# Block chunks of weights: four sums side by side, one rounding and one split

## The chip, the cores and the metric

The kernel runs on one core of a Trainium2 chip. The metric is the device time of one execution in microseconds. A profiled execution gives a span (first to last instruction of the program) and a trace of every engine: PE (matmul, with its weight loads as PEld), DVE (elementwise), ACT (copies, casts, activations), POOL and SP (which issues the loads from HBM).

## The reference

Two layers of a decoder trunk on 256 tokens of width 2048, all in float32. Layer 0 mixes stick-breaking attention and an SSD scan, layer 1 a causal mixture of dilated windows; each layer ends with a gated ConvFFN of inner width 5632.

```python
for layer in range(DEPTH):
    hn = rms_norm(h, mix_norm_w[layer])
    ...
    h = h + mix.astype(h.dtype)
    f = conv_ffn(rms_norm(h, ffn_norm_w[layer]), ffn_w_gate[layer], ffn_w_up[layer],
                 ffn_conv_w[layer], ffn_conv_b[layer], ffn_w_down[layer])
    h = h + f.astype(h.dtype)
return rms_norm(h, final_norm_w)
```

What the change touches is the product of activations with weights in two places: the value projection of layer 1 (`hn @ w_in`, its last third, in `odd`) and the last down projection (`... @ w_down` of layer 1, in `finish`).

## The kernel before

All weights stream once from HBM in chunks of 512 KB (128 partitions by 1024 floats). Each product is made of three terms: activations and weights are each held as a rounded part (high, of type fp32r) and a rest (low), and high*high, high*low and low*high are summed. So each chunk that lands in a `raw` buffer is prepared by ACT, which writes the rounded part, and DVE, which writes the rest, before PE may use it.

There are two kinds of chunk.

- A **plain chunk** goes through `prep` (lines 148 to 168): one load (L164), one cast on ACT of 1024 columns (L166), one subtraction on DVE (L167). PE uses it in `chan` (L242) or, in `finish`, in `plain` (L586).
- A **block chunk** goes through `pair_prep` (lines 473 to 506). It holds four blocks of 256 columns, and the product of a 2 by 2 block matrix is formed in seven block products in place of eight (`seven`, L534; 21 matmuls of 256 columns, with three terms each). Three blocks are used as they are (B11, B21, B22), and four sums of blocks (T1 to T4) are formed on DVE first (L492, L495, L496) in a buffer `tf`. PE takes them in the order B11, B21, B22, T1, T3, T2, T4.

Block chunks are used 51 times. 24 of them are in `odd`: its loop over p from 0 to 3 projects queries and keys of four heads in 16 plain chunks, with a chunk of the values after each second plain one; for p = 1, 2 and 3 these are block chunks. I number them 0 to 23 (0 to 7 for p = 1, and so on), and call the two plain chunks that PE uses just ahead of block chunk 9 by 9a and 9b. Attention for the heads (`dilated`: L850 to L883) and the values' sums (`combine`: L546 to L556) run between them, in generators that are stepped once a chunk. The other 27 are in `finish`, where plain and block chunks alternate.

Three pools set how far preparation runs ahead: `raw` has 4 buffers, `hl` 3 (one per chunk of either kind), and `ts` 2, for block chunks alone. `tf` has one. In a block chunk before the change, `hl` holds the B blocks (high, low) and T4; `ts` holds T1 to T3. A buffer is handed out again when its last reader is done, so the cast of B (L491) waits for PE to be done with the chunk that had the `hl` buffer, and a load waits for the last instruction that reads the `raw` buffer it gets.

The code does not set the order on an engine directly: a scheduler of the language places the instructions of each engine when the program is built, by its own estimate of when each can start, and decides there which buffer each chunk gets. On the chip each engine then runs its list strictly in that order, and SP issues loads in its own order.

Of the kernel before, what the change touches and what calls it, by code (L numbers as in the profile page):

```python
# [9 lines left out]
F32 = mybir.dt.float32  # L10
# [3 lines left out]
ALU = mybir.AluOpType  # L14

P = 128
T = 256
# [55 lines left out]
class Trunk:  # L73
# [399 lines left out]
    def pair_prep(self, src, off=OFF):  # L473

        nc = self.nc
        v = nc.vector
        raw = self.wraw.tile([P, CH * 272], F32, tag="raw", name=self.nm("raw"))[:, : 4 * T]
        hl = self.whl.tile([P, CH * 544], F32R, tag="hl", name=self.nm("hl"))  # L480
        ts = self.ph.tile([P, 128 + 6 * T], F32R, tag="ts", name=self.nm("ts"), bufs=2)
        cut = lambda t, o, n: t[:, off + o * T : off + (o + n) * T]
        b = cut(hl, 0, 3), cut(hl, 3, 3)
        t123 = cut(ts, 0, 3), cut(ts, 3, 3)
        t4 = cut(hl, 6, 1), cut(hl, 7, 1)
        nc.sync.dma_start(raw, src)
        blk = lambda t, i, n=1: t[:, i * T : (i + n) * T]
        two = lambda t: t.rearrange("p (i c) -> p i c", c=T)
        f = self.ph.tile([P, 4 * T], F32, tag="tf", name=self.nm("tf"), bufs=1)
        f123, f4 = blk(f, 0, 3), blk(f, 3)  # L490
        nc.scalar.copy(b[0], blk(raw, 0, 3))  # L491
        v.tensor_tensor(  # L492
            two(blk(f123, 0, 2)), two(blk(raw, 1, 2)), blk(raw, 3).unsqueeze(1).broadcast_to([P, 2, T]), ALU.subtract
        )
        v.tensor_tensor(blk(f123, 2), blk(raw, 2), blk(f123, 0), ALU.add)  # L495
        v.tensor_tensor(f4, blk(raw, 0), blk(f123, 2), ALU.subtract)  # L496
        v.tensor_tensor(b[1], blk(raw, 0, 3), b[0].bitcast(F32), ALU.subtract)  # L497
        nc.scalar.copy(t123[0], f123)  # L498
        nc.scalar.copy(t4[0], f4)
        v.tensor_tensor(t123[1], f123, t123[0].bitcast(F32), ALU.subtract)  # L500
        self.lo = v.tensor_tensor(t4[1], f4, t4[0].bitcast(F32), ALU.subtract)
        one = lambda t, i: (blk(t[0], i), blk(t[1], i))
        return {
            "B21": one(b, 0), "B11": one(b, 1), "B22": one(b, 2),
            "T1": one(t123, 0), "T3": one(t123, 1), "T2": one(t123, 2), "T4": t4,
        }

    def part(self, x, p, tt):
        return x[:, p * T + tt * P : p * T + (tt + 1) * P]
# [859 lines left out]
```

## Time and profile before

| | us |
|---|---|
| three runs | 2176.47, 2177.75, 2178.99 (median 2177.75) |
| the profiled execution | 2177.32 |
| its span, first to last instruction | 2175.5 |
| mean granted TensorE clock | 0.999 |
| `odd`, p = 1 to 3 (24 block chunks) | about 1155 to 1365 of the span |
| `finish`, block chunks 24 to 50 | about 1985 to 2160 of the span |

Every row of the timeline gives start, duration, engine, line, operation, what it writes and reads, and how often; in brackets stands the idle time ahead of it and what ended that. PE's matmuls are pipelined: the duration of one is its latency, and the distance between the starts of two is what it costs.

### The profile page before, as it was taken

The numbers are of one execution on the slowest core, as the hardware profiler recorded it, in microseconds if no ns is written. First come the engines' busy times: TensorE is split into PE (matmuls) and PEld (weight loads), VectorE is DVE, ScalarE is ACT, GpSimd is POOL, SyncE is SP. The second block draws the span as 40 slices with busy tenths as digits, with TensorE's granted clock in tenths as the row PEclk, the third lists the DMA queues.
The fourth block names the chain that finished last, engine by engine and source line by source line (L and its number), as shares of the span: only waits on it lengthen the run. The fifth ranks groups of instructions, "written<-read, shape, count | busy, mean of one in ns | idle before, by whom it ended". The sixth has DMA issues, their size and how long they took to land.

```text
span 2175.5 us, 34570 instructions
## 1 busy us (share of the span) xinstructions
PE 2164.5 (99%) x13335; PEld 1935.9 (89%) x13335; DVE 1595.9 (73%) x2518; ACT 1195.4 (55%) x1782; POOL 96.9 (4%) x107
## 2 busy tenths in 40 slices
PE   9999999999999999999999999999999999999998
PEld 8888888888888888888889999888888888888998
DVE  8688776766666665555578888767676767688997
ACT  7566554655555554444455655546555555555554
POOL 0000000101010100000000000000010101000000
PEclk9999999999999999999999999999999999999999
DMA  7754566666666666666665556666666666666665
GB/s 253 242 175 146 174 184 191 189 193 194 193 195 194 193 194 195 194 193 194 193 182 183 175 176 192 178 192 187 188 193 195 193 194 194 194 200 203 208 203 169
DMA packets 117717, 417.59 MB, mean 192 GB/s; under 512 B 13072, under 2 KB 15408, under 8 KB 117552
## 3 DMA queue, kind: packets, MB, share of 16 engines
q1 hardware_dynamic: 116352, 412.48, 62.4%
q8 instruction: 104, 1.70, 0.3%
q0 software_dynamic: 576, 2.10, 0.3%
q10 hardware_dynamic: 624, 0.81, 0.1%
q14 instruction: 61, 0.50, 0.1%
HBM read 413.22 MB, written 2.11 MB: 191 GB/s over the span
## 4 chain that ended last, share of the span: by engine, by line
PE 96%; DVE 2%; DMA 1%; ACT 0%; issue 0%; DVEq 0%
PE acc L242 77%; PE acc L586 5%; PE acc L519 3%; PE aux L534 3%; PE acc L534 2%; PE acc L252 1%; PE aux L519 1%; DMA raw<-in_wodv 1%; DVE hl L167 1%; PE acc L203 1%; PE acc L259 1%; PE aux L881 0%; PE acc L211 0%; PE aux L211 0%; PE aux L849 0%
## 5 line engine op out<-in xcount | busy, mean ns | idle before, releaser
L242 PE MATMUL acc<-x,hl 128*128 128x512 f32 (+1 forms) x7680 | 1324.3, 333 | 1.7 <-DVE hl L167 1.6
L242 PEld LDWEIGHTS acc<-x,hl 128*128 128x128 f32 x7680 | 1157.8, 188 | 152.0 <-DVE hl L167 2.2
L167 DVE TENSOR_TENSOR hl<-raw,hl 128x1024 fp32r<-128x1024 f32 x713 | 872.4, 1224 | 499.5 <-ACT hl L166 493.1
L166 ACT CAST hl<-raw 128x1024 fp32r<-128x1024 f32 x713 | 748.4, 1050 | 701.5 <-PE acc L242 476.5
L242 PE MATMUL acc<-act,hl 128*128 128x512 f32 (+1 forms) x1408 | 239.5, 332 | 0.0
L242 PEld LDWEIGHTS acc<-act,hl 128*128 128x128 f32 x1408 | 211.7, 188 | 27.7
L242 PE MATMUL acc<-o,hl 128*128 128x256 f32 (+1 forms) x1024 | 176.0, 333 | 0.0
L242 PEld LDWEIGHTS acc<-o,hl 128*128 128x128 f32 x1024 | 154.2, 188 | 20.1 <-ACT das L857 0.2
L301 ACT COPY ev<-acc 128x256 f32<-128x256 f32 x242 | 89.9, 373 | 140.1 <-PE acc L242 138.0
L747 POOL TENSOR_TENSOR cv<-cv,rbc 128x256 f32<-128x256 f32 x88 | 93.8, 1084 | 852.7 <-ACT cv L746 852.7
L586 PE MATMUL acc<-hl,act 128*128 128x256 f32 x924 | 110.4, 276 | 0.0
L586 PEld LDWEIGHTS acc<-hl,act 128*128 128x128 f32 x924 | 107.9, 188 | 0.3
L302 DVE TENSOR_TENSOR ev<-acc,ev 128x256 f32<-128x256 f32 x242 | 101.1, 420 | 3.1 <-ACT ev L301 1.7
L498 ACT CAST ts<-tf 128x768 fp32r<-128x768 f32 x51 | 42.7, 837 | 36.9 <-DVE tf L495 36.8
L519 PE MATMUL acc<-hl,act 128*128 128x512 f32 x264 | 60.0, 389 | 0.0
L491 ACT CAST hl<-raw 128x768 fp32r<-128x768 f32 x51 | 42.6, 836 | 29.9 <-issue 18.2
L519 PEld LDWEIGHTS acc<-hl,act 128*128 128x128 f32 x264 | 49.5, 188 | 10.3
L497 DVE TENSOR_TENSOR hl<-raw,hl 128x768 fp32r<-128x768 f32 x51 | 48.7, 954 | 4.2 <-ACT hl L491 4.0
L500 DVE TENSOR_TENSOR ts<-tf,ts 128x768 fp32r<-128x768 f32 x51 | 48.6, 953 | 2.2 <-ACT ts L498 2.2
L492 DVE TENSOR_TENSOR tf<-raw 128x512 f32<-128x512 f32 x51 | 35.2, 690 | 18.9 <-DMA raw<-in_wodv 15.0
L757 DVE TENSOR_TENSOR ev<-ev,cv 128x256 f32<-128x256 f32 x88 | 38.3, 437 | 10.2 <-POOL cv L747 1.5
L309 POOL MEMSET pad<- 128x2 f32 (+1 forms) x8 | 0.5, 100 | 928.1 <-DVE sum L122 928.1
(253 smaller groups left out, 1556.4 us busy)
## 6 DMA issues: line engine op xcount, KB each, us to landing
raw<-in_wg SPq DMA_DIRECT2D x176, 512.0 KB, 3.9
raw<-in_wu SPq DMA_DIRECT2D x176, 512.0 KB, 3.8
raw<-in_wd SPq DMA_DIRECT2D x176, 512.0 KB, 3.6
raw<-in_wev SPq DMA_DIRECT2D x76, 512.0 KB, 4.1
raw<-in_wod SPq DMA_DIRECT2D x64, 512.0 KB, 3.9
raw<-in_wevo SPq DMA_DIRECT2D x32, 512.0 KB, 3.6
raw<-in_wodv SPq DMA_DIRECT2D x32, 512.0 KB, 3.6
raw<-in_wodo SPq DMA_DIRECT2D x32, 512.0 KB, 4.3
```

The costliest lines, as they stand in the source:

```text
L166: nc.scalar.copy(hi, raw)
L167: self.lo = nc.vector.tensor_tensor(lo, raw, hi.bitcast(F32), ALU.subtract)
L242: self.mm = self.nc.tensor.matmul(accs[nt][:, :n], hl[w][:, k, nt * P : (nt + 1) * P], xs[k0 + k][:, :n], start=start and k == w == 0, sto ...
L301: nc.scalar.copy(t, acc[:, T:])
L302: nc.vector.tensor_tensor(t, acc[:, :T], t, ALU.add)
L497: v.tensor_tensor(b[1], blk(raw, 0, 3), b[0].bitcast(F32), ALU.subtract)
L498: nc.scalar.copy(t123[0], f123)
L500: v.tensor_tensor(t123[1], f123, t123[0].bitcast(F32), ALU.subtract)
L519: self.nc.tensor.matmul(row.rearrange("p (j c) -> p j c", c=T), self.part(a[k], p, tt), self.both(hl, w, k), start=start and i == k == 0, ...
L534: self.nc.tensor.matmul(to, x[p], w[b][q], start=n == 0 and i in start, stop=n == 2 and i in stop, skip_group_check=alone or i in m,)
L586: mm(block(accs, tt, j) if own is None else own[:, :T], x, both(hl, w, k)[:, j], start=first, stop=stop and k == 1 and i == 2 and j == hal ...
L747: nc.gpsimd.tensor_tensor(c, c, self.rbc, ALU.mult)
```

## The change

The four sums now lie side by side in the `hl` buffer, high and low, and are rounded by one ACT cast of 1024 columns and split by one DVE subtraction of 1024 columns. The B blocks move to `ts`. The products and their operands' values are the same.

```diff
-        b = cut(hl, 0, 3), cut(hl, 3, 3)
-        t123 = cut(ts, 0, 3), cut(ts, 3, 3)
-        t4 = cut(hl, 6, 1), cut(hl, 7, 1)
+        t = cut(hl, 0, 4), cut(hl, 4, 4)
+        b = cut(ts, 0, 3), cut(ts, 3, 3)
         nc.sync.dma_start(raw, src)
...
         nc.scalar.copy(b[0], blk(raw, 0, 3))
         v.tensor_tensor(
-            two(blk(f123, 0, 2)), two(blk(raw, 1, 2)), blk(raw, 3).unsqueeze(1).broadcast_to([P, 2, T]), ALU.subtract
+            two(blk(f, 0, 2)), two(blk(raw, 1, 2)), blk(raw, 3).unsqueeze(1).broadcast_to([P, 2, T]), ALU.subtract
         )
-        v.tensor_tensor(blk(f123, 2), blk(raw, 2), blk(f123, 0), ALU.add)
-        v.tensor_tensor(f4, blk(raw, 0), blk(f123, 2), ALU.subtract)
+        v.tensor_tensor(blk(f, 2), blk(raw, 2), blk(f, 0), ALU.add)
+        v.tensor_tensor(blk(f, 3), blk(raw, 0), blk(f, 2), ALU.subtract)
         v.tensor_tensor(b[1], blk(raw, 0, 3), b[0].bitcast(F32), ALU.subtract)
-        nc.scalar.copy(t123[0], f123)
-        nc.scalar.copy(t4[0], f4)
-        v.tensor_tensor(t123[1], f123, t123[0].bitcast(F32), ALU.subtract)
-        self.lo = v.tensor_tensor(t4[1], f4, t4[0].bitcast(F32), ALU.subtract)
+        nc.scalar.copy(t[0], f)
+        self.lo = v.tensor_tensor(t[1], f, t[0].bitcast(F32), ALU.subtract)
```

Of the changed kernel's lines, L489 is the cast of B and L495 its subtraction (L491 and L497 before), L490, L493 and L494 form the sums (L492, L495, L496 before), and L496 and L497 are the merged cast and subtraction. Lines behind `pair_prep` stand six lower: L528 is L534 before.

The list of every engine but SP and POOL changes, since the cast of B no longer needs an `hl` buffer and the scheduler places it, and what follows it, earlier. Three places:

**ACT, from block chunk 8 to 9b.** Before: `raw1678` holds the weights of block chunk 8, and `hl1673`, `hl1683` and `hl1685` are the plain chunks 8b, 9a and 9b.

```order
L166 CAST hl1673_11771<-raw1672_11770 128x1024
L546 COPY tc1661_11718<-acc1565_11045 128x256
L491 CAST hl1679_11798<-raw1678_11797 128x768
L499 CAST hl1679_11798<-tf1681_11801 128x256
L166 CAST hl1683_11833<-raw1682_11832 128x1024
L551 ACTIVATE vw1662_11719<-vw1662_11719,rcol1455_10383 128x512
L556 ACTIVATE vw1663_11720<-vw1663_11720,rcol1455_10383 128x512
L857 ACTIVATE das1668_11747,dam1669_11748<-das1668_11747,dam1669_11748 128x128 x2
L857 ACTIVATE das1668_11747,dam1669_11748<-das1668_11747,dam1669_11748 128x256 x2
L166 CAST hl1685_11854<-raw1684_11853 128x1024
```

After, over the same stretch; `raw1692` holds the weights of block chunk 9.

```order
L166 CAST hl1673_11755<-raw1672_11754 128x1024
L540 COPY tc1661_11702<-acc1565_11045 128x256
L496 CAST hl1679_11782<-tf1681_11785 128x1024
L489 CAST ts1694_11878<-raw1692_11876 128x768
L545 ACTIVATE vw1662_11703<-vw1662_11703,rcol1455_10383 128x512
L550 ACTIVATE vw1663_11704<-vw1663_11704,rcol1455_10383 128x512
L166 CAST hl1683_11815<-raw1682_11814 128x1024
L851 ACTIVATE das1668_11731,dam1669_11732<-das1668_11731,dam1669_11732 128x128 x2
L851 ACTIVATE das1668_11731,dam1669_11732<-das1668_11731,dam1669_11732 128x256 x2
L166 CAST hl1685_11836<-raw1684_11835 128x1024
```

The cast of block chunk 9 stands ahead of the casts of 9a and 9b and of the values and exponentials; before, it stood behind 9b. On DVE a little earlier the same happens: before, the list at block chunk 8 runs L492, L495 (its first sums), L167 of 8a; after, it runs L495 (low half of block chunk 8's B), L490, L493, L167 of 8a.

**DVE, block chunk 5.** Before; `raw1632` is block chunk 5's, `hl1625` and `hl1627` are 5a and 5b, `das` and `dam` belong to the attention's softmax.

```order
L850 TENSOR_TENSOR das1614_11379<-aux1616_11381,consts_93 128x384
L167 TENSOR_TENSOR hl1625_11455<-raw1624_11454,hl1625_11455 128x1024
L850 TENSOR_TENSOR das1614_11379<-aux1617_11385,consts_93 128x384
L492 TENSOR_TENSOR tf1635_11510<-raw1632_11506 128x512
L853 TENSOR_REDUCE dam1615_11380<-das1614_11379 128x2 x2
L495 TENSOR_TENSOR tf1635_11510<-raw1632_11506,tf1635_11510 128x256
L496 TENSOR_TENSOR tf1635_11510<-raw1632_11506,tf1635_11510 128x256
L860 RECIPROCAL dam1615_11380<-dam1615_11380 128x4
L863 TENSOR_TENSOR das1614_11379<-das1614_11379,dam1615_11380 128x2x128
L863 TENSOR_TENSOR das1614_11379<-das1614_11379,dam1615_11380 128x2x256
L167 TENSOR_TENSOR hl1627_11476<-raw1626_11475,hl1627_11476 128x1024
```

After, the same stretch.

```order
L490 TENSOR_TENSOR tf1635_11500<-raw1632_11496 128x512
L493 TENSOR_TENSOR tf1635_11500<-raw1632_11496,tf1635_11500 128x256
L495 TENSOR_TENSOR ts1634_11498<-raw1632_11496,ts1634_11498 128x768
L844 TENSOR_TENSOR das1614_11371<-aux1616_11373,consts_93 128x384
L844 TENSOR_TENSOR das1614_11371<-aux1617_11377,consts_93 128x384
L167 TENSOR_TENSOR hl1625_11445<-raw1624_11444,hl1625_11445 128x1024
L847 TENSOR_REDUCE dam1615_11372<-das1614_11371 128x2 x2
L494 TENSOR_TENSOR tf1635_11500<-raw1632_11496,tf1635_11500 128x256
L854 RECIPROCAL dam1615_11372<-dam1615_11372 128x4
L857 TENSOR_TENSOR das1614_11371<-das1614_11371,dam1615_11372 128x2x128
L857 TENSOR_TENSOR das1614_11371<-das1614_11371,dam1615_11372 128x2x256
L167 TENSOR_TENSOR hl1627_11466<-raw1626_11465,hl1627_11466 128x1024
```

Three instructions that read block chunk 5's weights now stand ahead of the scores, of 5a and of the softmax's maximum (L853, now L847).

**PE, block chunk 1.** Before; `hl1572` is the plain chunk 1a, and the products of block chunk 1 come 32 matmuls later.

```order
L534 MATMUL aux1564_11044<-hl1568_11048,x1236_8750 128x256 x3
L242 MATMUL acc1551_10970<-x1321_9516,hl1572_11083 128x512
L242 MATMUL acc1551_10970<-x1321_9516,hl1572_11083 128x256
L242 MATMUL acc1551_10970<-x1322_9521,hl1572_11083 128x512
L242 MATMUL acc1551_10970<-x1322_9521,hl1572_11083 128x256
```

After; `ts1581` is block chunk 1.

```order
L528 MATMUL aux1564_11044<-hl1568_11048,x1236_8750 128x256 x3
L242 MATMUL acc1551_10970<-x1321_9516,hl1572_11081 128x512
L242 MATMUL acc1552_10971<-x1321_9516,hl1572_11081 128x512
L528 MATMUL acc1565_11045<-ts1581_11134,x1240_8778 128x256 x3
L528 MATMUL aux1563_11043<-ts1581_11134,x1241_8783 128x256
L242 MATMUL acc1551_10970<-x1321_9516,hl1572_11081 128x256
L242 MATMUL acc1551_10970<-x1322_9521,hl1572_11081 128x512
```

Two products with the high half of 1a and four of block chunk 1 stand ahead of the first product with 1a's low half. Elsewhere PE's list is the same but for the buffers' names.

SP issues the same loads in the same order, but some get another `raw` buffer and so wait for other work. Block chunk 9's load waited for the split of 8b (L167) and now waits for the last sum of block chunk 8 (L494); the same holds for block chunks 5, 6, 7, 13, 14, 15, 17, 21, 22 and 23 with the one ahead of each. Block chunk 8's load waited for the split of 7b and now waits for that of 7a.

More of the change, by code (lines that the diff above doesn't have):

```diff
@@ L489, in pair_prep @@
         f = self.ph.tile([P, 4 * T], F32, tag="tf", name=self.nm("tf"), bufs=1)
-        f123, f4 = blk(f, 0, 3), blk(f, 3)
         nc.scalar.copy(b[0], blk(raw, 0, 3))
         v.tensor_tensor(
-            two(blk(f123, 0, 2)), two(blk(raw, 1, 2)), blk(raw, 3).unsqueeze(1).broadcast_to([P, 2, T]), ALU.subtract
+            two(blk(f, 0, 2)), two(blk(raw, 1, 2)), blk(raw, 3).unsqueeze(1).broadcast_to([P, 2, T]), ALU.subtract
         )
-        v.tensor_tensor(blk(f123, 2), blk(raw, 2), blk(f123, 0), ALU.add)
-        v.tensor_tensor(f4, blk(raw, 0), blk(f123, 2), ALU.subtract)
+        v.tensor_tensor(blk(f, 2), blk(raw, 2), blk(f, 0), ALU.add)
+        v.tensor_tensor(blk(f, 3), blk(raw, 0), blk(f, 2), ALU.subtract)
         v.tensor_tensor(b[1], blk(raw, 0, 3), b[0].bitcast(F32), ALU.subtract)
[L498 to L501, printed above, removed]
+        nc.scalar.copy(t[0], f)
+        self.lo = v.tensor_tensor(t[1], f, t[0].bitcast(F32), ALU.subtract)
         one = lambda t, i: (blk(t[0], i), blk(t[1], i))
[L503 to L506, printed above, removed]
+        out = {n: one(b, i) for i, n in enumerate(("B21", "B11", "B22"))}
+        return out | {n: one(t, i) for i, n in enumerate(("T1", "T3", "T2", "T4"))}
     def part(self, x, p, tt):
```

## The prediction

> **What bounds the kernel now.** I read the page's busy shares first, then the chain that ended last, then busy time by window for the two stages that the change touches.
>
> ```profile
> PE 2164.5 (99%) x13335; PEld 1935.9 (89%) x13335; DVE 1595.9 (73%) x2518; ACT 1195.4 (55%) x1782; POOL 96.9 (4%) x107
> PE 96%; DVE 2%; DMA 1%; ACT 0%; issue 0%; DVEq 0%
> core 0: us, PE busy (x) PEld busy (x) DVE busy (x) ACT busy (x) POOL busy (x), PEclk, DMA share, GB/s
> 1155.00:1365.00 210.00, 209.58 (x1409) 192.38 (x1408) 184.22 (x313) 125.21 (x225) 0.00 (x0) 1.00 0.59 182
> 1985.00:2160.00 175.00, 175.00 (x1485) 172.72 (x1484) 158.09 (x240) 99.79 (x137) 0.00 (x0) 1.00 0.65 201
> ```
>
> PE is busy 2164.5 of 2175.5 us and 96% of the last chain is PE. In the window of `odd` (first row) PE lacks 0.42 us of 210, in that of `finish` nothing, at full clock. The change leaves every matmul. So it can win only what PE waits for here, which the chain of waits in the window of `odd` gives (us in total, times, longest):
>
> ```profile
> DVE tf L492 <- DMA raw<-in_wodv: 15.0, 10, 3.1
> PEld acc L534 <- DVE hl L497: 0.7, 2, 0.4
> PEld acc L242 <- DVE ev L302: 0.4, 1, 0.4
> PE acc L534 <- DVE hl L497: 0.2, 1, 0.2
> PE acc L242 <- DVE ev L302: 0.2, 1, 0.2
> ```
>
> PE's four waits make 1.5 us. The 0.7 is the low half of B coming late at block chunks 8 and 16. The first row is as important: ten times DVE stood waiting at the head of its list for a block chunk's load, up to 3.1 us, and PE mostly had cover.
>
> **What the instructions cost.** Groups of one shape each, mean ns behind the bar:
>
> ```profile
> L167 DVE TENSOR_TENSOR hl<-raw,hl 128x1024 fp32r<-128x1024 f32 x713 | 872.4, 1224 | 499.5 <-ACT hl L166 493.1
> L497 DVE TENSOR_TENSOR hl<-raw,hl 128x768 fp32r<-128x768 f32 x51 | 48.7, 954 | 4.2 <-ACT hl L491 4.0
> L500 DVE TENSOR_TENSOR ts<-tf,ts 128x768 fp32r<-128x768 f32 x51 | 48.6, 953 | 2.2 <-ACT ts L498 2.2
> L501 DVE TENSOR_TENSOR hl<-tf,hl 128x256 fp32r<-128x256 f32 x51 | 21.4, 419 | 0.0
> L492 DVE TENSOR_TENSOR tf<-raw 128x512 f32<-128x512 f32 x51 | 35.2, 690 | 18.9 <-DMA raw<-in_wodv 15.0 <-DMA raw<-in_wd 3.0
> L498 ACT CAST ts<-tf 128x768 fp32r<-128x768 f32 x51 | 42.7, 837 | 36.9 <-DVE tf L495 36.8
> L499 ACT CAST hl<-tf 128x256 fp32r<-128x256 f32 x51 | 20.5, 403 | 1.1 <-DVE tf L496 1.1
> ```
>
> DVE's two subtractions cost 0.953 + 0.419 = 1.37 us; one of 1024 columns costs 1.22 as L167 does. ACT's two casts cost 0.837 + 0.403 = 1.24; one of 1024 costs 1.05 (the row of L166 at block chunk 1, below). That saves 0.15 us of DVE and 0.19 of ACT per block chunk, 51 times 7.6 and 9.7 us. **Both lie beside PE, so I cost the saving at nothing**, save where DVE was what PE waited for. The Trainium skill ("Perfetto Trace Analysis", section "Optimizing Scalar/DVE Operations") says that grouping helps if the engine is saturated, and that where it is not, but makes others wait, smaller instructions may let work finish sooner; by the first half the sum would be lower (rival C), by the second higher, and DVE's 184 of 210 us, with the ten waits above among its idle time, lies nearer to the second.
>
> **T123 comes later.** The merged cast waits for the fourth sum (0.42 us) and both operations are longer (0.21 and 0.27): T's low half is ready 0.5 to 0.9 us later. The tightest place is block chunk 1:
>
> ```profile
> 1166.35 0.96 DVE L500 TENSOR_TENSOR ts<-tf,ts 128x768 fp32r<-128x768 f32 x1 [0.44 <-ACT ts L498]
> 1169.01 1.18 PE L534 MATMUL acc<-ts,S 128*128 128x256 f32 x9
> ```
>
> The low half ends at 1167.31, PE takes it at 1169.01: 1.7 us of cover. Cost 0; without that cover each chunk would pay up to 0.9.
>
> **`finish`.** PE repeats every 5.10 us, and B's low half is 2.5 us ahead:
>
> ```profile
> 2021.45 0.95 DVE L497 TENSOR_TENSOR hl<-raw,hl 128x768 fp32r<-128x768 f32 x1
> 2024.92 0.50 PE L534 MATMUL aux<-hl,act 128*128 128x256 f32 x3
> ```
>
> Here the added wait (the merged cast for the fourth sum) delays what stands behind it by half a microsecond at most, against this 2.5. Cost 0. A round of sums, merged cast, merged split and plain split becomes 0.69 + 0.42 + 0.42 + 1.05 + 1.22 + 1.22 = 5.0 us, close to PE's 5.1; the bounds are 0 and 27 x 0.1 = 2.7, if handoffs between ACT and DVE made it 5.2.
>
> **The early cast of B in `odd`.** Here the order rows matter. The cast of B needs no `hl` buffer now, so it stands ahead of plain casts, and whatever is behind it waits until its load has landed. SP issues the same loads, so a load's issue moves only with the work that frees its buffer. Issue to landing of a 512 KB load in this window:
>
> ```profile
> DMA to landing us min/median/max: 3.4/3.9/5.2
> ```
>
> I reckon with 3.9. The Trainium skill ("SBUF — State Buffer", section "The DMA setup-cost knee (why "@ 1 MiB" ≠ asymptote)") fits a load as 2 us plus its bytes by 436 GB/s, an estimate of 3.2 us here; by it the casts would wait 0.7 us less and the sum below would be that of rival A. The row's least, 3.4, is above it, so the row decides.
>
> *Block chunks 8 and 16.*
>
> ```profile
> 1219.02 0.69 DVE L492 TENSOR_TENSOR tf<-raw 128x512 f32<-128x512 f32 x1 [3.07 <-DMA raw<-in_wodv]
> ...
> 1220.09 1.22 DVE L167 TENSOR_TENSOR hl<-raw,hl 128x1024 fp32r<-128x1024 f32 x1
> 1221.23 0.42 DVE L302 TENSOR_TENSOR ev<-acc,ev 128x256 f32<-128x256 f32 x1
> 1221.70 3.07 PE L242 MATMUL acc<-x,hl 128*128 128x512 f32 x16 [0.16 <-DVE ev L302]
> ```
>
> Before: DVE waits for the load until 1219.02, forms two sums, splits 8a, adds `ev`, which ends at 1221.65, and PE starts at 1221.70 with 0.16 us idle. After: the cast of B (0.84, 0.75 until its successor may start) and its subtraction (0.95, 0.87) come first on that way: 1.6 us later. The load waits for 7a's split in place of 7b's, one subtraction and its waits earlier; but the plain load issued ahead of it shares the DMA engines, so I take 0.6 us of gain, between 0 and 1.6. So PE waits **1.0 us at each of the two, 2.0** (0 to 3.2). In exchange the late low half of B is gone: **-0.7**.
>
> *Block chunks 9 and 17.* DVE's list is full from that landing on.
>
> ```profile
> 1230.20 1.22 DVE L167 TENSOR_TENSOR hl<-raw,hl 128x1024 fp32r<-128x1024 f32 x1
> ...
> 1232.94 1.23 DVE L167 TENSOR_TENSOR hl<-raw,hl 128x1024 fp32r<-128x1024 f32 x1
> 1231.55 1.09 PE L242 MATMUL acc<-x,hl 128*128 128x512 f32 x5
> ```
>
> The splits of 9a and 9b end at 1231.42 and 1234.17. PE needs the first at its second product, 1231.55 + 0.23 = 1231.78, the second 2.73 later at 1234.5 (16 products at the rate of the 32 further down: 5.45 us): 0.35 us of cover. After, DVE does 1.22 - 0.95 - 0.42 + 0.69 = 0.5 us more before them (the first sum of 9 now precedes them) and all is 1.0 later from block chunk 8; PE itself is 1.0 later, less half of the 0.7 us of waits that go. Beyond the cover that is 0.5 + 0.35 - 0.35 = 0.5 at worst; as DVE's rows overlap by 0.1 each, I take **0.3 each, 0.6** (0 to 1.6).
>
> *Block chunks 5, 13, 21.* B's cast and three readers of its load stand ahead of the softmax maximum, whose exponentials stand ahead of 5b's cast.
>
> ```profile
> 1186.19 0.33 SPq L164 DMA_DIRECT2D raw<-in_wod  x1
> 1189.19 0.33 SPq L486 DMA_DIRECT2D raw<-in_wodv  x1
> ...
> 1194.29 1.01 DVE L853 TENSOR_REDUCE dam<-das 128x2 f32<-128x256 f32 x2
> ...
> 1197.80 1.22 DVE L167 TENSOR_TENSOR hl<-raw,hl 128x1024 fp32r<-128x1024 f32 x1
> 1197.20 5.62 PE L242 MATMUL acc<-x,hl 128*128 128x512 f32 x32
> 1202.65 0.51 PE L534 MATMUL acc<-hl,x 128*128 128x256 f32 x3
> ```
>
> 5b's split ends at 1199.02; PE needs it at 1197.20 + 2.73 + 0.23 = 1200.16: 1.1 us of cover. Block chunk 5's load was issued at 1189.19, when 4b's split was done; 5b's at 1186.19, when 4a's was. After: it waits for block chunk 4's last sum, which DVE forms behind 4a's split and one `ev` (0.42) that PE releases, so it is issued at about 1187.1 and lands at 1191.0. Then come first sum, second sum, B's subtraction, two scores (0.55 each) and 5a's split. The maximum starts at about 1195.0 (0.7 late, covered) with a landing of 3.9, at 1196.3 (2.0 late) with 5.2. Between none and 0.9 I take **0.3 each, 0.9**.
>
> *Block chunk 1.* 1a's cast goes behind B's cast and the exponentials, and its split behind two additions of L388.
>
> ```profile
> 1155.03 1.05 ACT L166 CAST hl<-raw 128x1024 fp32r<-128x1024 f32 x1 [0.85 <-ACT S L467]
> 1162.90 0.75 DVE L388 TENSOR_TENSOR o<-aux,o 128x256 fp32r<-128x256 f32 x2
> 1162.53 5.62 PE L242 MATMUL acc<-x,hl 128*128 128x512 f32 x32
> ```
>
> If the split follows L388 as that stands, it ends at 1163.6 + 1.2 = 1164.8; if ACT's earlier start pulls L388 in by 0.7, at 1164.1. PE's list puts six products ahead of the first low one, so it is needed at about 1162.53 + 2 x 0.23 + 4 x 0.11 = 1163.4, later by what those take more. I take **1.0** (0 to 1.4). Other blocks have over 2 us: **0.3** in all (0 to 2).
>
> **The sum** is 2.0 - 0.7 + 0.6 + 0.9 + 1.0 + 0.3 = **+4.1 us** on the profiled execution of 2177.32 (span 2175.5 and 1.8 outside it): **2181.4**. The median of the runs, 2177.75, is 0.4 above that execution; I don't add it. About 0.2%, 4.4 us, is what a measurement of this kernel can tell from no change: 2173.4 to 2182.1.
>
> **The rivals.**
>
> *A: the cover holds.* All new waits vanish behind earlier loads and PE's 1.5 us of waits may go too: 2175.8 to 2178.8. For it: ten waits of DVE, 15.0 us, cost PE almost nothing before. Against: 8a's split was already the last to arrive (0.16 idle on `ev`).
>
> *B: late landings at the head of ACT's list (slower).* The cast of B holds ACT, so plain splits come late, so `raw` buffers come free late, so the next loads are issued late. It decides where a landing takes over 0.4 us more than 3.9 (1.1 of cover less 0.7 at block chunk 5). At 5.2 us each of the ten places named or summed above loses up to 1.3; at half of them 6.5 more: 2187.9. For it: landings do take up to 5.2, and L492 did wait for them up to 3.1 us. Against: where PE is late, cover grows for all that follows.
>
> *C: DVE's relief counts in full.* If PE moved as fast as DVE lets it, 51 x 0.15 = 7.6 us would go: 2169.7. Against: PE's idle time and waits in both windows make under 2 us. (This is the first half of the rule cited above from the Trainium skill, "Perfetto Trace Analysis".)
>
> That the change doesn't do what it says is excluded: ACT and DVE each lose an instruction per block chunk in the order.
>
> **How the numbers follow.** With every term at its low bound the sum is -0.7, with PE's other waits gone -1.5; with every term at its high bound it is 3.2 - 0.7 + 1.6 + 2.7 + 1.4 + 2 + 2.7 = 12.9, or 2190.2. The forecast, with its own range 2178.8 to 2182.1, has 0.42; A 0.15; B 0.40 (2182.1 to 2195); C 0.03. Thus faster 0.03, same 0.57, slower 0.40. The range reaches from A's low end, 2176, to 2190, where C and the top quarter of B are left out (0.13; the rest is for what I overlooked).
>
> **What would show it.** Right: L496 and L497 at 1.05 and 1.22 us; no wait of PE on B's subtraction at 8 and 16, but one on `ev` or on L167 of 8a and 16a near 1 us; PE's idle time in 1155 to 1365 at about 4 to 5 us; none in `finish`; waits of ACT's L489 for the load. Wrong: waits of PE on the merged subtraction (T's cover misjudged), any wait in `finish`, or PE's idle time there spread over blocks that I gave nothing.

## The result and the profile after

The changed kernel takes 2191.2 us (median of six runs, 2188.97 to 2192.48) against 2178.2 before (six runs, 2176.47 to 2178.99): **slower by 0.59%, ratio 1.0059 with a 95% interval of 1.0049 to 1.0070**, 13.0 us. The profiled execution took 2188.97 us with a span of 2187.2, 11.7 more than before. The forecast of 2181.4 was too low and the time lies above the range of 2176 to 2190; rival B, 2187.9, came nearest.

The page of the changed kernel, busy shares and the chain that ended last:

```profile
PE 2169.3 (99%) x13335; PEld 1937.3 (89%) x13335; DVE 1594.5 (73%) x2467; ACT 1185.7 (54%) x1731; POOL 97.1 (4%) x107
PE 89%; DVE 5%; DMA 4%; ACT 1%; issue 1%; DVEq 0%; ACTq 0%
```

DVE and ACT are busy for less time, with 51 instructions fewer each: 1.4 and 9.7 us. (Busy time counts rows that overlap once; the rows of the helper's own groups on DVE add up to 8.2 us less.) But the chain is no longer PE alone: 11% of it now runs through DVE, DMA, ACT and issue, which had about 3%. Busy time by window, the two stages (a little longer than before, since the stages are):

```profile
1155.00:1375.00 220.00, 212.68 (x1405) 192.06 (x1404) 182.88 (x288) 121.52 (x200) 0.00 (x0) 1.00 0.54 173
1985.00:2175.00 190.00, 189.94 (x1559) 185.72 (x1558) 164.33 (x221) 98.48 (x114) 0.00 (x0) 1.00 0.63 195
```

In `odd` PE now lacks 7.3 us of 220 where it lacked 0.42 of 210, at the same clock; in `finish` it is as full as before. The waits in the window of `odd` (us in total, times, longest):

```profile
ACT ts L489 <- DMA raw<-in_wodv: 50.0, 22, 4.4
...
DVE tf L490 <- DMA raw<-in_wodv: 11.4, 8, 1.9
DVE ts L495 <- ACT ts L489: 10.5, 4, 3.8
...
PEld acc L242 <- DVE hl L167: 6.2, 9, 1.3
...
PE acc L242 <- DVE hl L167: 3.6, 6, 1.0
PEld acc L242 <- DVE ev L302: 3.5, 4, 1.8
...
PE acc L242 <- DVE ev L302: 2.6, 2, 1.6
...
PEld acc L242 <- ACT hl L166: 1.3, 2, 0.7
```

The first row is the new one: ACT stood 22 times, 50 us in all, with the cast of B (L489) at the head of its list, waiting for a load. Before, the cast of B waited for no load that the view shows; DVE did (15.0 us, ten times), and PE mostly had cover. What PE waits for is not B at all: it is the low half of *plain* chunks (L167), and `ev`, which stand behind.

To put a size on each place, I take the distance between the starts of successive matmuls less its usual value (227 ns for 512 columns, 113 for 256). Summed over `odd`, this excess was about 2.7 us before and is about 13.3 now, and in `finish` 0.8 and 1.5: together some 11 more, of the span's 11.7 us. (The sums shift by up to 1 us with which distances are counted as usual; the single waits in the table don't.)

| place | excess before, us | after | my term |
|---|---|---|---|
| ahead of 8a and 16a | 0.3 and 0 | 1.16 and 1.81 | +2.0 |
| B of 8 and 16, inside | 0.33 and 0.26 | 0 | -0.7 |
| 9a, 9b and 17a, 17b | 0 | 1.49 and 0.59 | +0.6 |
| 5b, 13b, 21b | 0 | 0, 1.68, 1.79 | +0.9 |
| block chunk 1 | 0 | 0.40 | +1.0 |
| behind 10, 18 (L865) | 0 | 0.40 and 0.19 | in "others", +0.3 |

Three places as rows. Block chunk 8, timelines of ACT, DVE and PE of the changed kernel:

```profile
1218.26 0.83 ACT L489 CAST ts<-raw 128x768 fp32r<-128x768 f32 x1 [3.29 <-DMA raw<-in_wodv]
1219.00 1.04 ACT L166 CAST hl<-raw 128x1024 fp32r<-128x1024 f32 x1
...
1219.13 0.96 DVE L495 TENSOR_TENSOR ts<-raw,ts 128x768 fp32r<-128x768 f32 x1 [2.90 <-ACT ts L489]
1220.00 0.68 DVE L490 TENSOR_TENSOR tf<-raw 128x512 f32<-128x512 f32 x1
1220.72 0.42 DVE L493 TENSOR_TENSOR tf<-raw,tf 128x256 f32<-128x256 f32 x1
1221.06 1.22 DVE L167 TENSOR_TENSOR hl<-raw,hl 128x1024 fp32r<-128x1024 f32 x1
1222.20 0.42 DVE L302 TENSOR_TENSOR ev<-acc,ev 128x256 f32<-128x256 f32 x1
...
1222.67 1.54 PE L242 MATMUL acc<-x,hl 128*128 128x512 f32 x7 [0.99 <-DVE ev L302]
```

The load landed at 1218.24, 0.7 earlier than before, as reckoned (0.6); but cast and low half of B now come ahead of the sums, 8a's split and `ev`, and PE starts 8a at 1222.67 where it started at 1221.70.

Block chunk 13, the same engines:

```profile
1266.31 0.83 ACT L489 CAST ts<-raw 128x768 fp32r<-128x768 f32 x1 [3.76 <-DMA raw<-in_wodv]
...
1270.83 0.40 ACT L851 ACTIVATE das<-das,dam 128x128 f32<-128x128 f32 x1 [2.73 <-DVE dam L847]
...
1272.60 1.03 ACT L166 CAST hl<-raw 128x1024 fp32r<-128x1024 f32 x1
...
1273.88 1.22 DVE L167 TENSOR_TENSOR hl<-raw,hl 128x1024 fp32r<-128x1024 f32 x1
...
1275.16 2.08 PE L242 MATMUL acc<-x,hl 128*128 128x256 f32 x11 [0.98 <-DVE hl L167]
```

One late load goes down the whole column: the cast of B waits 3.76 us, DVE's scores and maximum come behind B's subtraction, the exponentials behind the maximum, 13b's cast behind the exponentials, 13b's split behind that, and PE waits for it.

At block chunk 9 the way is shorter (timelines of ACT and DVE):

```profile
1228.55 0.83 ACT L489 CAST ts<-raw 128x768 fp32r<-128x768 f32 x1 [4.44 <-DMA raw<-in_wodv]
...
1231.59 1.23 DVE L167 TENSOR_TENSOR hl<-raw,hl 128x1024 fp32r<-128x1024 f32 x1 [0.41 <-ACT hl L166]
```

Its load took 5.55 us to land (3.65 before). ACT stood 4.44 us at the cast of B, 9a's cast came behind it, and 9a's split, for which PE waits 0.69 us, waited for that cast.

### The profile page after: what moved, and what is told of

Its sections match the earlier page's. It is cut to its first block, busy times and chain, and to the rows that moved or that the text cites. A ratio compares the mean times of both kernels' runs of the same rounds, so it can differ in the third digit from the quotient of the medians.

```text
span 2187.2 us, 34493 instructions
## 1 busy us (share of the span) xinstructions
PE 2169.3 (99%) x13335; PEld 1937.3 (89%) x13335; DVE 1594.5 (73%) x2467; ACT 1185.7 (54%) x1731; POOL 97.1 (4%) x107
## 4 chain that ended last, share of the span: by engine, by line
PE 89%; DVE 5%; DMA 4%; ACT 1%; issue 1%; DVEq 0%; ACTq 0%
PE acc L242 74%; PE acc L580 3%; DMA raw<-in_wodv 3%; PE acc L513 3%; PE aux L528 2%; DVE hl L167 1%; PE acc L528 1%; PE acc L252 1%; PE aux L513 1%; DMA raw<-in_wd 1%; PE acc L203 1%; PE acc L259 1%; DVE tf L490 0%; DVE ts L495 0%; PE acc L211 0%
## 5 line engine op out<-in xcount | busy, mean ns | idle before, releaser
L167 DVE TENSOR_TENSOR hl<-raw,hl 128x1024 fp32r<-128x1024 f32 x713 | 871.5, 1223 | 491.9 <-ACT hl L166 485.5
L489 ACT CAST ts<-raw 128x768 fp32r<-128x768 f32 x51 | 42.7, 836 | 103.7 <-DMA raw<-in_wodv 50.0
L496 ACT CAST hl<-tf 128x1024 fp32r<-128x1024 f32 x51 | 53.5, 1049 | 47.6 <-DVE tf L494 34.6
L497 DVE TENSOR_TENSOR hl<-tf,hl 128x1024 fp32r<-128x1024 f32 x51 | 62.4, 1223 | 13.6 <-ACT hl L496 13.1
L495 DVE TENSOR_TENSOR ts<-raw,ts 128x768 fp32r<-128x768 f32 x51 | 48.6, 953 | 17.6 <-ACT ts L489 16.9
L513 PEld LDWEIGHTS acc<-hl,act 128*128 128x128 f32 x264 | 49.5, 188 | 10.3
L490 DVE TENSOR_TENSOR tf<-raw 128x512 f32<-128x512 f32 x51 | 35.0, 686 | 15.0 <-DMA raw<-in_wodv 11.4
```

What stands on the lines that cost most here:

```text
L167: self.lo = nc.vector.tensor_tensor(lo, raw, hi.bitcast(F32), ALU.subtract)
L496: nc.scalar.copy(t[0], f)
L497: self.lo = v.tensor_tensor(t[1], f, t[0].bitcast(F32), ALU.subtract)
L513: self.nc.tensor.matmul(row.rearrange("p (j c) -> p j c", c=T), self.part(a[k], p, tt), self.both(hl, w, k), start=start and i == k == 0, ...
```

## The experiments

Theory "place": the loss comes from the cast of B standing early in ACT's list, which the move of B from `hl` to `ts` allows. Rivals: "merge" (the longer operations cost it) and later "buffers" (raw buffers handed out in another order bunch the loads). All ratios are against runs of the kernel before on the same chip.

**e1: the merge alone.** B stays in `hl`, the four sums lie in a wider `ts`.

```diff
-        t = cut(hl, 0, 4), cut(hl, 4, 4)
-        b = cut(ts, 0, 3), cut(ts, 3, 3)
+        t = cut(ts, 0, 4), cut(ts, 4, 4)
+        b = cut(hl, 0, 3), cut(hl, 3, 3)
```

> Keeps the merged cast and the merged subtraction of the four sums, but leaves the B blocks in the hl buffer as before and puts the sums into a wider ts; the cast of B then waits for an hl buffer again and stands behind the plain casts in ACT's list. Theory 'place' (the loss comes from the cast of B standing early in ACT's list, waiting for its load): 2177 to 2179 us, PE's waits in odd below 3 us. Rival 'merge' (the loss comes from the merged operations themselves, which are longer and wait for the fourth sum): about 2191 us.

2178.31 us against 2178.1, ratio 1.0000 (0.9991 to 1.0010). The merge costs nothing, and brings nothing. PE's excess in `odd` is 2.7 us as before.

**e2: the move alone.** Buffers as in the change, two casts and two subtractions as before.

```diff
-        nc.scalar.copy(t[0], f)
-        self.lo = v.tensor_tensor(t[1], f, t[0].bitcast(F32), ALU.subtract)
+        nc.scalar.copy(blk(t[0], 0, 3), blk(f, 0, 3))
+        nc.scalar.copy(blk(t[0], 3), blk(f, 3))
+        v.tensor_tensor(blk(t[1], 0, 3), blk(f, 0, 3), blk(t[0], 0, 3).bitcast(F32), ALU.subtract)
+        self.lo = v.tensor_tensor(blk(t[1], 3), blk(f, 3), blk(t[0], 3).bitcast(F32), ALU.subtract)
```

> The other half alone: B in ts and the sums in hl as in the change, but rounded and split by two operations each as before. Place: 2189 to 2193 us, with the same waits of PE on 8a, 13b, 16a, 21b. Merge: about 2178 us.

2189.69 us, ratio 1.0051 (1.0036 to 1.0066). So nearly the whole loss comes with the move of B. In its waits ACT stands even longer at the cast of B, and PE waits for the same things:

```profile
ACT ts L489 <- DMA raw<-in_wodv: 56.5, 22, 5.2
...
PEld acc L242 <- DVE hl L167: 6.8, 8, 1.3
...
PEld acc L242 <- DVE ev L302: 2.4, 2, 1.5
```

**e3: an edge that holds the cast of B back.** The changed kernel, with the cast of B placed on ACT behind the cast of the plain chunk ahead of it.

```diff
-        nc.scalar.copy(b[0], blk(raw, 0, 3))
+        with self.tc.issue_after(self.hi.ins):
+            nc.scalar.copy(b[0], blk(raw, 0, 3))
```

> The changed kernel in full, with one ordering edge: the cast of B may stand in ACT's list only behind the cast of the plain chunk ahead of it. Buffers as in the change. Place: 2177 to 2179 us. Merge: about 2191. A third theory, 'buffers' (the loads are issued in bunches because the raw buffers are freed by other work, wherever the cast stands): above 2185 us.

2196.96 us, ratio 1.0088 (1.0072 to 1.0103): slower than the change itself, which only the open-ended "above 2185" of "buffers" allows, and the edge is no test of that theory: as built, the kernel with the edge hands out the `raw` buffers of `odd` in the turn of before, not in that of the change. The trace parts it in two. In `odd` the excess fell from 13.3 to about 8.0 us. In `finish` it rose from 1.5 to about 10.3, in a wait that the change itself hardly has (waits in the window of `finish`):

```profile
ACT hl L497 <- DVE tf L495: 70.6, 24, 3.1
DVE hl L498 <- ACT hl L497: 29.4, 27, 1.2
...
PEld aux L529 <- DVE hl L498: 8.7, 18, 0.6
```

There the edge puts the sums' cast and split on a chain of handoffs that is longer than PE's 5.1 us: PE waits in 18 of the 27 rounds, 0.3 to 0.6 us each, and those rounds take 5.8 us. This is the kind of loss for which the prediction set a bound of "5.2" a round, brought about by my edge and not by the change.

**e4 and e5: the new form in one stage only.** The old helper for the calls of the other stage (the edit of e4; e5 does the same in `finish`).

```diff
-                    self.seven(rows, m, self.pair_prep(src, OFF + 32), two, ...
+                    self.seven(rows, m, self.pair_prep_old(src, OFF + 32), two, ...
```

> The new form only for the 27 block chunks of finish, the old form for the 24 of odd. Place: 2177.5 to 2179.5 us (the profile after shows PE's lost time in finish up by about 0.7 us). Merge: 27 of 51 chunks, about 2185 us.

> The new form only for the 24 block chunks of odd, the old form in finish. If the loss lies in odd: 2189 to 2191 us. If finish holds a good part of it: below 2186.

In `finish` alone 2180.64 us, ratio 1.0011 (1.0001 to 1.0020); in `odd` alone 2188.8, ratio 1.0051 (1.0036 to 1.0066). So about 10.9 us of the loss lie in `odd` and about 2.5 in `finish`, where e4 lies above the 2179.5 that was expected at most. In e4's trace PE waits in `finish` on the merged subtraction, once or twice, and ACT's cast of B waits for loads there too:

```profile
ACT ts L489 <- DMA raw<-in_wd: 51.6, 24, 3.5
...
PEld aux L563 <- DVE hl L497: 1.0, 2, 0.7
```

**e6: the edge in `odd` only.**

> As e3, but the edge (cast of B behind the plain cast ahead of it on ACT) only for the block chunks of odd; finish as in the change. Theory 'place alone': 2178 to 2180 us. Theory 'place and buffers' (about half of the loss is the cast's place, the rest is that the raw buffers which B's new place hands out bunch the loads, so that block chunks 8 and 16 land late wherever the cast stands; e3's trace has 8.0 us of PE's lost time in odd against 13.3 of the change): about 2186 us, with PE waiting over 1 us ahead of 8a and of 16a.

2187.12 us, ratio 1.0039 (1.0026 to 1.0053): 4.1 us of the 13 come back, no more. "Place alone" falls. ACT hardly waits for loads any more (0.2 us in `odd`), but DVE does (21.4 us, 11.4 in the change), 8a and 16a wait as much as ever, and the load of block chunk 8 is why (timelines of SP, DVE and PE of e6):

```profile
1218.84 0.33 SPq L164 DMA_DIRECT2D raw<-in_wod  x1
1220.31 0.33 SPq L485 DMA_DIRECT2D raw<-in_wodv  x1
1221.18 0.33 SPq L164 DMA_DIRECT2D raw<-in_wod  x1
...
1225.88 0.69 DVE L494 TENSOR_TENSOR tf<-raw 128x512 f32<-128x512 f32 x1 [3.57 <-DMA raw<-in_wodv]
...
1228.55 1.66 PE L242 MATMUL acc<-x,hl 128*128 128x512 f32 x8 [0.79 <-DVE ev L302]
```

It took 5.5 us to land (1220.31 to 1225.79), with a load 1.5 us ahead of it and the load of 9a 0.9 us behind. Before, these gaps were 2.3 and 1.2 and it took 4.5; in e1 1.8 and 2.0, and 4.4. The `raw` buffers go round in fixed turn in `odd` in e6, as before; 9a's load takes block chunk 7's buffer, and is early because the low half of that chunk's B, the last to read it, now runs ahead of the merged subtraction.

**e8: an edge on DVE only.** The low half of B in `odd` behind the plain split, ACT's cast free.

> The changed kernel with the edge on DVE instead: the low half of B in odd may stand only behind the subtraction of the plain chunk ahead of it; ACT's cast of B is free to stand early. If what costs is ACT held at the head of its list by the load: 2188 to 2191 us. If it is DVE's early reading of B (the low half ahead of the plain splits): 2184 to 2187, as e6 by 'place and buffers'.

2191.98 us, ratio 1.0064 (1.0047 to 1.0081): nothing gained. This makes e8 the counterpart of e6. As built, the two have the same lists on PE and SP, the same turn of the `raw` buffers and, but for 16 places around block chunks 10, 11, 18 and 19, the same list on DVE; what differs is where ACT casts B, and the medians lie 4.9 us apart (the intervals touch). So the cast's place on ACT costs by itself. And since e8 has the `raw` turn of before and loses as much as the change, the change's own turn isn't needed for the loss. That DVE's order counts beside the cast, e12 shows. (The trace of e8 is of its fastest execution, 2187.73 us; the other three took 2191.92 to 2192.11. That of e6 is of its slowest, 2190.85.)

**e9: the old form at block chunks 8 and 16.**

> The changed kernel, with the old form at block chunks 8 and 16 alone. PE's waits of the changed kernel ahead of 8a, 16a and in 9 and 17 (1.16 + 1.81 + 0.69 + 0.80 + 0.13 + 0.46 = 5.1 us) go and the old 0.7 comes back: about 2186.8 us if places 9 and 17 only inherit the delay of 8 and 16; 2188.9 if just 8 and 16 recover.

2186.77 us, ratio 1.0041 (1.0026 to 1.0056), as the first case said, but not by its sum: the waits ahead of 8a and 16a are gone and those at 9 fell from 1.49 to 0.55 us, but at 17 they did not (0.59 and 0.62), 5b now waits 0.80, and the wait behind block chunks 10 and 18 (L900 there, L865 in the change) grew from 0.4 and 0.2 to 1.0 and 1.1 us. The number agrees partly by accident, and doesn't tell how much 9 and 17 inherit.

**e12: e6, and the buffer freed as late as before.** In `odd` the low half of B also stands behind the merged subtraction.

```diff
+        if behind:
+            with self.tc.issue_after(self.lo.ins):
+                self.lo = v.tensor_tensor(b[1], blk(raw, 0, 3), b[0].bitcast(F32), ALU.subtract)
```

> As e6 (edge on ACT in odd), and in odd the low half of B also stands behind the merged subtraction on DVE, so the raw buffer of a block chunk comes free about 1.2 us later, as it did before. In e6 the load of 9a was issued 0.9 us behind that of block chunk 8 (1.2 before the change, 2.0 in e1) and block chunk 8's took 5.5 us to land (4.5 and 4.4). Theory 'early freeing' (a raw buffer freed early sends a load that no one needs soon into the back of the one PE waits for): 2179 to 2182 us, block chunk 8's load landing in about 4.5 us, PE's wait ahead of 8a and 16a below 0.4 us. Rival (the loads are late for another reason): 2186 us or more.

2181.66 us, ratio 1.0015 (1.0006 to 1.0025): 9.5 of the 13 us are back, by two ordering edges, with B and the sums in the buffers where the change puts them. (The `raw` buffers of `odd` go round as in e6 and as before.) Against e6, whose lists on ACT and PE are nearly and on SP wholly the same, the later low half, with the merged subtraction now ahead of it, is worth 5.4 us. The load of 9a now goes out 3.3 us behind that of block chunk 8, which itself is 2.2 us behind the load ahead (1.5 in e6) and lands in 4.6 us, and 8a doesn't wait. 16a does still, 1.16 us, against the expectation of under 0.4, and B's low half is late at 8 and 16 again:

```profile
PEld acc L536 <- DVE ts L505: 2.1, 3, 0.9
...
PEld acc L242 <- DVE ev L302: 1.2, 1, 1.2
```

**e10: the change with the raw buffers in fixed turn.** The cast of B stands early.

```diff
-        raw = self.wraw.tile([P, CH * 272], F32, tag="raw", ...
+        raw = self.wraw.tile([P, CH * 272], F32, tag=self.slot(), ...
```

> The changed kernel, with the four raw buffers handed out in fixed turn, as they were before the change in odd; the cast of B stands early. If the other buffers are what matters: 2183 to 2186 us. If the early cast of B is: 2189 us or more, since a block chunk's load then waits for the split of the plain chunk before last, which itself stands behind the cast of B.

2185.79 us, ratio 1.0032 (1.0019 to 1.0045): 5.4 of the 13 us come back, in the range of "other buffers". But the edit did more than it was meant to do: SP's list is another one, with the load of 9a ahead of that of block chunk 8, and likewise at 5, 6, 13, 16 and 21 (SP's timeline; three plain loads, those of 8a, 8b and 9a, where there were two):

```profile
1208.21 6.32 SPq L169 DMA_DIRECT2D raw<-in_wod  x3
1215.34 0.33 SPq L490 DMA_DIRECT2D raw<-in_wodv  x1
```

So the run doesn't tell the buffers' turn from the loads' order; e8, with a fixed turn and SP's order of before, gains nothing. ACT's wait at the cast of B falls from 50.0 to 21.7 us, and 13b and 21b no longer wait; 8a, 16a and both plain chunks of 9 and 17 still do.

## Why the prediction was wrong

- **PE is the bound, T's cover holds, the saving hides** (cost 0): right in `odd`, and e1 shows it by itself, with a ratio of 1.0000. In `finish` PE waits once on the merged subtraction (0.3 us), which the prediction had named as a sign of being wrong.
- **The way of the loss**: right, but for the share of ACT at 9. The early cast of B, in `odd`, at 8, 16, 9, 17, 5-like places and 1, with PE waiting on `ev` and L167, as the last part of the prediction lists. e2 shows that the move of B does it and not the merge. For 9 and 17 the working followed DVE alone and left out that ACT would stand at the cast of B ahead of 9a's cast; there it was ACT's wait of 4.44 us that made 9a's split late.
- **The change waits that go** (-0.7): right; 0.33 and 0.26 us are gone.
- **The step that failed: "I reckon with 3.9".** I took the landing time of before for that of after. A load's landing varies with how close behind the load ahead it is issued (the table at the end), and the change moves exactly that: casts held at the head of ACT's list and buffers freed in another order send the loads out in bunches. The loads of plain and block chunks in the window of `odd`, before and then after (DMA issues: x, KB each, median us from issue to landing):

```profile
raw<-in_wod SPq DMA_DIRECT2D x44, 512.0 KB, 4.1
raw<-in_wodv SPq DMA_DIRECT2D x22, 512.0 KB, 3.7
```

```profile
raw<-in_wod SPq DMA_DIRECT2D x44, 512.0 KB, 3.6
raw<-in_wodv SPq DMA_DIRECT2D x22, 512.0 KB, 4.4
```

  So the plain loads got faster, and the loads of block chunks, at which ACT now stands, got slower. Of the 72 loads in the window 10 were issued within 1.6 us of the one ahead before, 29 after. Block chunk 16's took 3.95 us before and 5.11 after, those of 13 and 21 about 4.9, that of 9 5.55. The places sort by it: at 5 (4.07) there was no wait, at 17 (4.10) 0.59 us and at 8 (4.62) 1.16; at 9, 13, 16 and 21 the waits were 1.49 to 1.81. This is rival B's price, which I gave 0.40 where the forecast had 0.42; its ground "landings do take up to 5.2" was the right one, and I didn't ask what would make them.
- **The second failure: terms for one block taken for its likes.** For block chunk 5 the working holds almost to the digit: load issued at 1186.78 (reckoned 1187.1), landed at 1190.85 (1191.0), no wait at 5b. At 13, relative to PE's start on the plain chunk ahead, the load was issued 1.1 us later than that working and took 1.0 longer: the last sum of block chunk 12, which frees its buffer, stood behind a plain split that was itself late behind the cast of B:

```profile
1256.70 0.83 ACT L489 CAST ts<-raw 128x768 fp32r<-128x768 f32 x1 [2.32 <-DMA raw<-in_wodv]
```

  That cast, of block chunk 12, stood 2.32 us (the one of block chunk 4 1.17). The delay feeds the next load, as rival B says. So 0.3 each became 0, 1.68 and 1.79; 9 and 17 with 0.6 became 2.1, and 8 and 16 with 2.0 became 3.0. Block chunk 1, which has no predecessor of its kind to inherit from but 0, cost 0.4 instead of 1.0.
- **`finish`** (0, at most 2.7): e4 measures +2.5 (0.2 to 4.4). The place is the bound's but its mechanism is not shown to be: in the profiles PE waits only once or twice, on the merged subtraction, where a load of B came late; the handoffs of a round did not fall short in the change itself, only in e3.
- **Rival A** fell: cover didn't hold. **Rival C** fell: e1 has all of DVE's relief and no gain. (The Trainium skill, "Perfetto Trace Analysis", section "Optimizing Scalar/DVE Operations", says that grouping can help throughput if the engine is saturated, and that breaking up instructions may let work finish sooner where an engine isn't saturated but holds others up. Neither shows here: e1 groups and gains nothing, and e2 keeps the smaller pieces and loses as the change does.)
- **What stays open.** e6 gives 4.1 us and e12 9.5; of e12's remaining 3.4 us e4 accounts for about 2.5, in `finish`. What the turn of the `raw` buffers is worth by itself no run shows, since e10 also changes the order of the loads. That early freeing by itself makes block chunk 8's load late is shown by spacing and landing in e6 and e12, not by a kernel in which nothing else differs: e12 also moves the merged subtraction forward, and there the load ahead of block chunk 8's is further away as well. 16a's wait in e12 is unexplained. A fifth raw buffer, which would ask for loads earlier, was not tried: the kernel's memory has no room for it.

No version beats the kernel before. e1 equals it with 102 instructions fewer.

## What to carry to other kernels

When an edit moves a tile to another pool, ask first which wait goes: a wait for a buffer also keeps an instruction back, and without it a scheduler puts the instruction where its estimate of a load allows, at the head of a strict list, where one late load holds everything behind. Reckon a load's landing from the gaps to its neighbours in the new order, and not from the median of the old; and where a place recurs, follow the delay from one round into the next before the first round's term is multiplied. To merge operations without this risk, keep each tile in the pool that paced it (e1).

## What the runs showed of the hardware

A 512 KB load's time to land goes with the gap to the load ahead of it. From the issue and landing times of the 424 loads issued between 1155 and 1365 us, in the traces of before, after, e1, e2, e3 and e6:

| issued behind the load ahead by | loads | median us to land | 10th to 90th percentile |
|---|---|---|---|
| 3.5 us or more | 152 | 3.57 | 3.46 to 3.89 |
| 2.5 to 3.5 us | 70 | 3.65 | 3.52 to 4.39 |
| 1.8 to 2.5 us | 53 | 4.24 | 3.67 to 4.69 |
| under 1.8 us | 149 | 4.60 | 4.29 to 5.49 |
| of these, with another within 1.0 us behind | 6 | 5.35 | 4.76 to 5.59 |

(The estimate of 3.2 us by the fit in the Trainium skill, "SBUF — State Buffer", section "The DMA setup-cost knee (why "@ 1 MiB" ≠ asymptote)", lies below all of these loads.)

The last row looks as if a load issued *behind* another delayed it, by some 0.8 us against the row above. It is six loads, and block chunk 8's in e6 (5.5 us) is one of them. Against it: 37 loads of the same traces that were 1.8 us or more behind the load ahead were also followed within 1.0 us, and they landed in 3.34 to 3.93 us, median 3.62. So a follower alone delayed nothing; whether it does when the load ahead is close too is not shown. Block chunk 8's in e12 (4.6 us, 2.2 behind the load ahead) fits the table without it.
